# Seven block products in both ConvGLU layers, with sums of weight blocks formed by adding transfers

## The chip, the core and the metric

The kernel runs on one core of a Trainium2 chip. A core has five engines with a queue each: PE (TensorE, matrix products), DVE (VectorE), ACT (ScalarE), POOL (GpSimd) and SP (SyncE, which here only issues transfers). Each queue is worked off in order; engines wait for one another through semaphores. Operands lie in SBUF (128 partitions), products land in PSUM (eight banks of 128 x 512 float32). The metric is the device time of one execution in microseconds. Three runs of the kernel before gave 1870.25, 1871.61 and 1875.65, median 1871.61.

## What is computed

A two-layer diffusion backbone on 512 latent tokens and 256 context tokens of width 1024. Layer 0 mixes tokens with windowed attention, layer 1 with a bidirectional gated recurrence (HGRN2), and each layer ends in a ConvGLU, which is what the change touches:

```python
def conv_glu(h, w_up, conv_w, conv_b, w_down):
    gate, val = jnp.split(h @ w_up, 2, axis=-1)
    return (jax.nn.silu(dwconv3(gate, conv_w, conv_b)) * val) @ w_down
...
        hx2 = rms_norm(x, norm2_g[layer]) * (1.0 + sc2) + sh2
        x = x + g2 * conv_glu(hx2, ffn_w_up[layer], ffn_conv_w[layer], ffn_conv_b[layer], ffn_w_down[layer])
        if not last:
            ctx = ctx + cg1 * yc
...
            ctx = ctx + cg2 * conv_glu(hc2, ffn_w_up[layer], ffn_conv_w[layer], ffn_conv_b[layer], ffn_w_down[layer])
    return x
```

`w_up` is 1024 x 5632 (2816 gate columns and 2816 value columns), `w_down` 2816 x 1024. Layer 0 works on latent and context tokens, layer 1 on latent tokens only. All is float32.

## The kernel before

Features lie on partitions, tokens along the free dimension. To keep float32 accuracy with the faster float32r products, every operand is split into a high and a low part: ACT rounds a copy (`wh`, `hn[:, 0]`), DVE subtracts it from the source (`wl`, `hn[:, 1]`), and PE forms three products, high-high, high-low and low-high (`mm_steps`, L170; `product`, L188).

Weights come through `load_raw` (L90): SP transfers them into a tile `wr` of 2048 float32 a partition, of which there are two buffers, shared by all weight loads and by the 1 MB pieces of `ada_w` (`ada_steps`, L306). Split parts go to slots of `operand` (L84): 512 columns each, from a rotation of pools. In layer 0's ConvGLU these are `ws0` (4 slots) and `wsC` (2); in layer 1's `ws0` 4, `wsC` 2, `wsD` 2 and `wsE` 2.

The ConvGLU (`ffn`, L958) goes in rounds of hidden tiles of 128 (L31: six rounds in layer 0, three of 8, 7 and 7 in layer 1; 22 tiles in each layer). In a round, `up` (L973) makes each hidden tile's gate and value, multiplies, convolves and gates; one tile of the next round is made ahead; then the round's tiles go through `w_down` (L1006 to L1023). In layer 0 `up` also draws one step of the `ada_w` product for layer 1 (`side`).

Layer 0 uses a scheme of seven block products in place of eight (Winograd's form of Strassen's): `load_pair` (L125) treats the 1024 x 256 weight block of a hidden tile as 2 x 2 blocks: `a11`, `a12` (gate columns, inner features 0 to 511 and 512 to 1023), `a21`, `a22` (value columns, likewise). DVE forms four sums (`total`, L136): s1 = a21 + a22, s3 = a11 - a21, s2 = s1 - a11, s4 = a12 - s2, the last three in place in `wr`, s1 in the tile `s1` of pool `tmpA`, which has one buffer (two in layer 1's pool `tmpB`). Seven operands of 512 columns are split (L140, L141). The activations are split in two token halves of 386, and `halves` and `combos` (L365, L384) make seven operand sets `hs` from sums of their blocks, done when the residual stream is complete. `gate_pair` (L914) runs the seven products of 12 matmuls each (4 inner tiles, 3 part products), in the order 0, 1, 3, 6, 2, 5, 4 (0, 1, 3, 2, 4, 6, 5 for the first tile), into three PSUM banks Z, Y and V, copies intermediate sums out with ACT, adds with DVE (L925), and multiplies by the row factor `R` on DVE and, for the value half, on POOL (L926).

Layer 1 uses plain products (`gate_plain`, L898): for gate and value each eight inner tiles, three part products and two column ranges (256 and 258 tokens), 96 matmuls a hidden tile, with four split operands a tile from `load_w` (L99) and activations scaled and split once (`scaled`, L355, called from `hgrn_out`, L1274). Its multiplications by `R` are four DVE instructions that read PSUM (L912).

The order of the instructions on each engine comes from a planner, which simulates the program; `high_priority(offset=W_AHEAD)` lets the weight preparation run ahead of its place in the program.

Of the kernel before, what the change touches and what calls it, by code (L numbers as in the profile page):

```python
# [68 lines left out]
def f(t):  # L69
    return t.bitcast(F32)  # L70


class Kernel:
# [51 lines left out]
    def load_pair(self, parts, tmp):  # L125


        nc = self.nc
        raw, n = self.load_raw(parts)
        q = n // 4  # L130
        a11, a12, a21, a22 = (raw[:, i * q:(i + 1) * q] for i in range(4))
        s1 = tmp.tile([P, 512], F32, tag="s1", name="s1")[:, 0:q]
        ops = [tuple(t[:, 0:q] for t in self.operand()) for _ in range(7)]

        def total(o, x, y, op):
            nc.vector.tensor_tensor(o, x, y, op=op)  # L136
            return o

        def parts(i, src):
            nc.scalar.activation(ops[i][0], src, AF.Copy)  # L140
            nc.vector.tensor_tensor(ops[i][1], src, f(ops[i][0]), op=ALU.subtract)  # L141


        with self.tc.high_priority(offset=W_AHEAD):
            parts(0, a11)
            parts(1, a12)
            total(s1, a21, a22, ALU.add)
            s3 = total(a21, a11, a21, ALU.subtract)
            s2 = total(a11, s1, a11, ALU.subtract)
            parts(3, s2)  # L150
            parts(6, s3)
            parts(2, s1)
            parts(5, a22)
            s4 = total(a12, a12, s2, ALU.subtract)
            parts(4, s4)
        return ops
# [227 lines left out]
    def combos(self, ys, kk, hs, late=False):  # L384

        nc = self.nc
        (b11, b12), (b21, b22) = ys

        def put(i, src):
            nc.scalar.activation(hs[i][:, 0, kk], src, AF.Copy)  # L392
            nc.vector.tensor_tensor(hs[i][:, 1, kk], src, f(hs[i][:, 0, kk]), op=ALU.subtract)

        def diff(o, x, y, eng=nc.vector):
            eng.tensor_tensor(o, x, y, op=ALU.subtract)
            return o

        if late:
            t3 = diff(b22, b22, b12)  # L400
            t4 = diff(b21, b21, b11, nc.gpsimd)
            put(5, diff(b21, t4, t3))
# [114 lines left out]
    def row_factor(self, acc, lat_only, tmp, pp, tag, width, R, sh, dg):  # L517
# [18 lines left out]
        if R.shape[1] > TW:  # L536
            nc.vector.memset(R[:, TW:], sh)

# [358 lines left out]

    def gate_plain(self, ft, ops, hn, G, gg, R, rows, half, tmp, bank):  # L898


        nc = self.nc
        act = lambda k: (hn[:, 0, k], hn[:, 1, k])
        cols = ((0, 256), (256, C0))
        for j, dst in enumerate((G[:, 1:1 + C0], gg)):
            ps = [bank("pd")[:, 0:hi - lo] for lo, hi in cols]
            for _ in self.mm_steps(ops[j], range(KT), act, [(o, lo) for o, (lo, _) in zip(ps, cols)]):
                pass
            for _ in rows:
                pass

            for o, (lo, hi) in zip(ps, cols):
                nc.vector.tensor_tensor(dst[:, lo:hi], o, R[:, lo:hi], op=ALU.mult)  # L912

    def gate_pair(self, ft, ops, hs, G, gg, R, rows, half, tmp, bank):  # L914
# [10 lines left out]
        add = lambda o, x, y: nc.vector.tensor_tensor(o, x, y, op=ALU.add)  # L925
        times = lambda eng, o, x, y: eng.tensor_tensor(o, x, y, op=ALU.mult)  # L926
# [6 lines left out]
        nc.scalar.activation(g[2], Z, AF.Copy)  # L933
        next(rows, None)
        if ft == 0:
# [13 lines left out]
        add(g[3], g[3], t2)  # L949
        add(g[2], g[2], V)  # L950
# [7 lines left out]
    def ffn(self, l, hs, R, rows, lat_only, tmp, acp, bk, gp, done, side=None):  # L958
        nc, a = self.nc, self.a
        wup, wdn = a["ffn_w_up"][l], a["ffn_w_down"][l]  # L960
        half = C0 // 2 if lat_only else hs[0].shape[3]
# [11 lines left out]
        def up(ft):  # L973

            ws_ = [self.wcols(wup, ft * P, P), self.wcols(wup, DFF + ft * P, P)]
            ops = self.load_w(ws_) if lat_only else self.load_pair(ws_, tmp)
# [5 lines left out]
            (self.gate_plain if lat_only else self.gate_pair)(ft, ops, hs, G, gg, R, rows, half, tmp, bank)  # L982
# [291 lines left out]
    def hgrn_out(self, part, hn, acc, tmp, pj):  # L1274
        nc = self.nc
        self.shifts(1, 1, hn)
        wout = self.a["hgrn_w_out"][0]
        oh = part[0]
        act = lambda k: (oh[:, 0, k], oh[:, 1, k])
        for dp in range(KT // 2):  # L1280
# [6 lines left out]
            for j in range(2):  # L1287
# [14 lines left out]
    def run(self, stop=99):  # L1302
# [80 lines left out]
        self.hgrn_out(part, hn, acc, ot, pj)  # L1383
# [3 lines left out]
        R = Rp.tile([P, C0], F32, tag="R", name="R2")  # L1387
# [23 lines left out]
        self.ffn(1, hn, R, rows, True, tmp, acp, bk, gp, done1)  # L1411
# [41 lines left out]
```

## Time and profile before

| what | value |
|---|---|
| median of the three runs | 1871.61 us |
| the profiled execution, device time | 1872.88 us |
| its span in the profile | 1871.1 us |
| granted TensorE clock, mean | 0.988 |
| layer 0's ConvGLU | 425 to 970 us of the span |
| layer 1's ConvGLU | 1481 to 1871 us |

The span is what the profile's rows add up to; 1.8 us of the execution lie outside it. The rows used here are those of the page (busy time by engine, the chain of work that ended last, groups of instructions, transfers with the median time from issue to landing), the list of that chain in order of time, the timeline of single queues, and busy times of each engine in chosen stretches of the span. A row of a group has the line, engine, operation, output and inputs, shape and count, then busy time in us, mean ns of one, and the idle time before them with what ended it.

### The profile page before, as it was taken

Reading aid. Unit: us, or ns where it says so; the run is one execution under the profiler, and the core shown is the slowest. Engines: PE = TensorE matmul, PEld = TensorE weight load, DVE = VectorE, ACT = ScalarE, POOL = GpSimd, SP = SyncE. Lnnn points to the kernel's source line nnn. Section 1 sums busy time; section 2 is a strip of 40 time slices with the busy share of each in tenths; the row PEclk is TensorE's granted clock in tenths of the full one; section 3 lists DMA queues with packets and bytes.
Section 4 is the critical chain, followed back from the end, with each engine's and each line's share of the span. In section 5 each row is a group of like instructions: output and inputs, shape, how many; then the busy total and the mean of one; then the engine's idle time right before and its main releaser. Section 6 shows DMA issues by size and latency. Waiting matters only on the chain.

```text
span 1871.1 us, 32302 instructions
## 1 busy us (share of the span) xinstructions
PE 1801.3 (96%) x13326; PEld 1576.9 (84%) x13326; DVE 1214.1 (65%) x2243; ACT 754.7 (40%) x1478; POOL 247.4 (13%) x233
## 2 busy tenths in 40 slices
PE   6999999998999999999998999999998999999998
PEld 4976786787888888989887888988886799899997
DVE  5575667466867686766777676777676655455462
ACT  4354555465534252434354333333332443233332
POOL 1233333103201000101013101111110200000000
PEclk9999999998999999999998999999999999999999
DMA  9204104232333333233313212122220332333321
GB/s 309 66 23 158 47 24 169 68 102 68 124 113 102 113 124 113 91 113 124 113 61 90 58 35 58 35 57 58 57 69 24 90 91 91 90 96 96 92 82 65
DMA packets 204416, 166.44 MB, mean 89 GB/s; under 512 B 5149, under 2 KB 198254, under 8 KB 199150
## 3 DMA queue, kind: packets, MB, share of 16 engines
q1 hardware_dynamic: 196608, 160.47, 27.8%
q10 hardware_dynamic: 7662, 3.92, 0.7%
q8 instruction: 105, 1.72, 0.4%
q14 instruction: 41, 0.34, 0.1%
HBM read 162.27 MB, written 2.10 MB: 88 GB/s over the span
## 4 chain that ended last, share of the span: by engine, by line
PE 87%; DVE 5%; DMA 4%; issue 2%; ACT 1%; POOL 1%; SPq 0%; ACTq 0%; POOLq 0%; DVEq 0%
PE dn L170 15%; PE pd L170 13%; PE pZ L188 8%; PE pf L170 8%; PE pV L188 4%; PE pjq L598 4%; PE pv L170 4%; PE ao L170 4%; PE ho L170 3%; PE pq L170 3%; PE pv L824 2%; PE pt L816 2%; PE ada L309 2%; PE pY L188 2%; PE pgate L170 2%; PE kv L598 2%
## 5 line engine op out<-in xcount | busy, mean ns | idle before, releaser
L117 ACT ACTIVATE wh<-wr 128x512 fp32r<-128x512 f32 (+1 forms) x320 | 193.0, 618 | 452.3 <-DMA wr<-in_ffn_w_up 74.8
L118 DVE TENSOR_TENSOR wl<-wr,wh 128x512 fp32r<-128x512 f32 (+1 forms) x320 | 223.6, 705 | 140.3 <-ACT wh L117 138.3
L170 PE MATMUL dn<-g,wh 128*128 128x512 f32 (+1 forms) x1056 | 263.3, 357 | 2.2 <-ACT g L995 2.2
L170 PE MATMUL pd<-hn,wh 128*128 128x256 f32 (+1 forms) x1408 | 227.3, 284 | 0.9 <-issue 0.9
L170 PEld LDWEIGHTS dn<-g,wh 128*128 128x128 f32 x1056 | 175.4, 189 | 32.7 <-ACT g L995 2.8
L170 PEld LDWEIGHTS pd<-hn,wh 128*128 128x128 f32 x1408 | 194.2, 190 | 2.5 <-issue 2.3
L188 PE MATMUL pZ<-hs,wh 128*128 128x386 f32 x704 | 185.2, 345 | 3.0 <-ACT wh L140 1.5
L170 PE MATMUL dn<-g,wl 128*128 128x512 f32 (+1 forms) x528 | 159.4, 356 | 0.0
L140 ACT ACTIVATE wh<-wr 128x512 fp32r<-128x512 f32 x132 | 81.6, 628 | 167.9 <-DMA wr<-in_ffn_w_up 47.4
L170 PE MATMUL pd<-hn,wl 128*128 128x256 f32 x704 | 141.8, 283 | 0.0
L188 PEld LDWEIGHTS pZ<-hs,wh 128*128 128x128 f32 x704 | 128.0, 190 | 15.7 <-ACT wh L140 4.4
L141 DVE TENSOR_TENSOR wl<-wr,wh 128x512 fp32r<-128x512 f32 x132 | 94.0, 717 | 53.6 <-ACT wh L140 53.5
L170 PE MATMUL pf<-hn,wh 128*128 128x512 f32 (+1 forms) x512 | 119.3, 349 | 9.7 <-DVE xc L1023 8.8
L188 PE MATMUL pZ<-hs,wl 128*128 128x386 f32 x352 | 119.4, 343 | 2.2 <-DVE wl L141 2.2
L926 POOL TENSOR_TENSOR gg<-gg,R 128x772 f32<-128x772 f32 x22 | 53.9, 2449 | 458.3 <-DVE gg L925 446.6
L170 PEld LDWEIGHTS pd<-hn,wl 128*128 128x128 f32 x704 | 109.0, 190 | 0.0
L1023 DVE SCALAR_TENSOR_TENSOR xl<-dn,mod,xl 128x512 f32<-128x512 f32 x72 | 53.9, 748 | 73.7 <-PE dn L170 73.6
L170 PEld LDWEIGHTS dn<-g,wl 128*128 128x128 f32 x528 | 87.4, 188 | 14.8
L170 PEld LDWEIGHTS pf<-hn,wh 128*128 128x128 f32 x512 | 80.9, 192 | 22.5 <-ACT wh L117 9.1
L188 PE MATMUL pV<-hs,wh 128*128 128x386 f32 x352 | 92.2, 341 | 5.0 <-ACT hs L392 5.0
L598 PE MATMUL pjq<-wh,hn 128*128 128x256 f32 x384 | 77.8, 291 | 0.0
L188 PEld LDWEIGHTS pZ<-hs,wl 128*128 128x128 f32 x352 | 66.7, 190 | 6.6 <-DVE gg L925 3.4
(299 smaller groups left out, 3807.1 us busy)
## 6 DMA issues: line engine op xcount, KB each, us to landing
wr<-in_ffn_w_up SPq DMA_DIRECT2D x88, 512.0 KB, 5.1
wada<-in_ada_w SPq DMA_DIRECT2D x40, 1024.0 KB, 4.8
wr<-in_hgrn_w_in SPq DMA_DIRECT2D x40, 512.0 KB, 4.2
ar<-in_ada_w SPq DMA_DIRECT2D x32, 256.0 KB, 7.1
wr<-in_ffn_w_down SPq DMA_DIRECT2D x16, 512.0 KB, 4.1
wr<-in_ffn_w_down SPq DMA_DIRECT2D x8, 896.0 KB, 4.7
wr<-in_attn_w_in SPq DMA_DIRECT2D x6, 1024.0 KB, 8.1
wr<-in_attn_w_out SPq DMA_DIRECT2D x8, 512.0 KB, 4.9
```

The costliest lines, as they stand in the source:

```text
L117: nc.scalar.activation(wh, src, AF.Copy)
L118: nc.vector.tensor_tensor(wl, src, f(wh), op=ALU.subtract)
L140: nc.scalar.activation(ops[i][0], src, AF.Copy)
L141: nc.vector.tensor_tensor(ops[i][1], src, f(ops[i][0]), op=ALU.subtract)
L170: nc.tensor.matmul(o, lhsT=wt, rhs=at[:, t0:t0 + o.shape[1]], start=(first and n == 0 and i == 0), stop=(last and n == len(ks) - 1 and i = ...
L188: self.nc.tensor.matmul(ps, lhsT=wt, rhs=at, start=(first and k == 0 and i == 0), stop=(k == nk - 1 and i == 2), skip_group_check=not first)
L309: nc.tensor.matmul(ps[32 * j:32 * j + 32, 0:512], lhsT=self.cs[:, k, :], rhs=raw[:, j * 512:(j + 1) * 512], start=(k == 0), stop=(k == KT ...
L598: nc.tensor.matmul(out, lhsT=x, rhs=y[:, wk], start=(start and k == 0 and j == 0), stop=(stop and k == KT - 1 and j == 2))
L816: nc.tensor.transpose(pt[:, j * P:(j + 1) * P], pr[j][:, b * P:(b + 1) * P], self.ident)
L824: nc.tensor.matmul(pv[a * HD:(a + 1) * HD, 0:256], lhsT=V[:, tl, g, :], rhs=pT[:, a * 256:(a + 1) * 256], start=(b == 0), stop=(b == len(t ...
L926: times = lambda eng, o, x, y: eng.tensor_tensor(o, x, y, op=ALU.mult)
L1023: nc.vector.scalar_tensor_tensor(x[:, d], o, self.modc(l, v, 5, d), x[:, d], op0=ALU.mult, op1=ALU.add)
```

## The change

`load_pair` no longer uses DVE for the four sums. SP loads the block `a11` a second time, into the tile that was s1's and is now called `s3`, and POOL issues four transfers from SBUF to SBUF that add to their destination, each of 128 x 512 float32:

```diff
-        s1 = tmp.tile([P, 512], F32, tag="s1", name="s1")[:, 0:q]
+        s3 = tmp.tile([P, 512], F32, tag="s1", name="s3")[:, 0:q]
...
-        def total(o, x, y, op):
-            nc.vector.tensor_tensor(o, x, y, op=op)
+        def more(o, x):
+            nc.gpsimd.dma_start(out=o, in_=x, accum_op=ALU.add)
             return o
...
-            parts(0, a11)
-            parts(1, a12)
-            total(s1, a21, a22, ALU.add)
-            s3 = total(a21, a11, a21, ALU.subtract)
-            s2 = total(a11, s1, a11, ALU.subtract)
-            parts(3, s2)
-            parts(6, s3)
-            parts(2, s1)
-            parts(5, a22)
-            s4 = total(a12, a12, s2, ALU.subtract)
-            parts(4, s4)
+            nc.sync.dma_start(out=s3.rearrange("p (k m) -> p k m", m=P), in_=parts[0][:, 0:4])
+            parts_(0, a11)
+            parts_(1, a12)
+            more(s3, a21)
+            s1 = more(a21, a22)
+            s2 = more(a11, s1)
+            parts_(3, s2)
+            parts_(6, s3)
+            parts_(2, s1)
+            parts_(5, a22)
+            s4 = more(a12, s2)
+            parts_(4, s4)
```

Only sums are formed (s3 = a11 + a21, s1 = a21 + a22, s2 = a11 + s1, s4 = a12 + s2): the second row of blocks enters with its sign turned. The signs are put right on the side of the activations and of the results: `put` in `combos` takes a factor for operands 2 and 3 and two differences are turned round, and `gate_pair` copies two results with a factor of -1 and subtracts where it added:

```diff
-        put(2, t1)
+        put(2, t1, -1.0)
         t2 = diff(b22, b22, t1)
-        put(3, t2)
+        put(3, t2, -1.0)
         yield
-        put(5, diff(b21, b21, t2))
+        put(5, diff(b21, t2, b21))
...
-        nc.scalar.activation(g[2], Z, AF.Copy)
+        nc.scalar.activation(g[2], Z, AF.Copy, scale=-1.0)
...
-        add(g[3], g[3], t2)
-        add(g[2], g[2], V)
+        less(g[3], t2)
+        less(g[2], V)
```

Layer 1 takes the same scheme, with token halves of 258 (514 columns and two of padding). `gate_plain` goes; `hgrn_out` makes the seven operand sets instead of the one split of the activations:

```diff
-        half = C0 // 2 if lat_only else hs[0].shape[3]
+        half = hs[0].shape[3]
...
-            ws_ = [self.wcols(wup, ft * P, P), self.wcols(wup, DFF + ft * P, P)]
-            ops = self.load_w(ws_) if lat_only else self.load_pair(ws_, tmp)
+            ops = self.load_pair([self.wcols(wup, ft * P, P), self.wcols(wup, DFF + ft * P, P)], tmp)
...
-            (self.gate_plain if lat_only else self.gate_pair)(ft, ops, hs, G, gg, R, rows, half, tmp, bank)
+            self.gate_pair(ft, ops, hs, G, gg, R, rows, half, tmp, bank)
...
-        self.shifts(1, 1, hn)
...
+            some.append(self.combos(self.halves(1, 1, dp, 258, True, tmp, ("y0", "y1"), 4), dp, hs))
+            next(some[-1])
             for d in (dp, dp + 4):
-                self.scaled(1, 1, d, hn, True)
                 self.square_acc(d, acc, True, tmp, "sg", first=(d == 0), eng=nc.gpsimd)
+        for rest in some:
+            for _ in rest:
+                pass
...
-        hn = self.hn_tile(hc, "hn3", C0)
+        hs1 = hc.tile([P, 7, 2, 4, 258], F32R, tag="hs", name="hs3")
+        hs = [hs1[:, i] for i in range(7)]
...
-        R = Rp.tile([P, C0], F32, tag="R", name="R2")
+        R = Rp.tile([P, 516], F32, tag="R", name="R2")
```

The row factor's padding columns are filled in layer 1 too. Rounds, pools, the number of `wr` buffers and the priorities stay as they were.

More of the change, by code (lines that the diff above doesn't have):

```diff
@@ L131, in load_pair, with parts_ @@
         a11, a12, a21, a22 = (raw[:, i * q:(i + 1) * q] for i in range(4))
-        s1 = tmp.tile([P, 512], F32, tag="s1", name="s1")[:, 0:q]
+        s3 = tmp.tile([P, 512], F32, tag="s1", name="s3")[:, 0:q]
         ops = [tuple(t[:, 0:q] for t in self.operand()) for _ in range(7)]
-        def total(o, x, y, op):
-            nc.vector.tensor_tensor(o, x, y, op=op)
+        def more(o, x):
+            nc.gpsimd.dma_start(out=o, in_=x, accum_op=ALU.add)
             return o
-        def parts(i, src):
+        def parts_(i, src):
             nc.scalar.activation(ops[i][0], src, AF.Copy)
@@ L389, in combos, with put @@
         (b11, b12), (b21, b22) = ys
-        def put(i, src):
-            nc.scalar.activation(hs[i][:, 0, kk], src, AF.Copy)
-            nc.vector.tensor_tensor(hs[i][:, 1, kk], src, f(hs[i][:, 0, kk]), op=ALU.subtract)
+        def put(i, src, sign=1.0):
+            nc.scalar.activation(hs[i][:, 0, kk], src, AF.Copy, scale=sign)
+            if sign > 0:
+                nc.vector.tensor_tensor(hs[i][:, 1, kk], src, f(hs[i][:, 0, kk]), op=ALU.subtract)
+            else:
+                nc.vector.scalar_tensor_tensor(hs[i][:, 1, kk], src, sign, f(hs[i][:, 0, kk]), op0=ALU.mult, op1=ALU.subtract)
         def diff(o, x, y, eng=nc.vector):
@@ L401, in combos @@
             t4 = diff(b21, b21, b11, nc.gpsimd)
-            put(5, diff(b21, t4, t3))
+            put(5, diff(b21, t3, t4))
             put(6, t3)
@@ L535, in row_factor @@
         nc.vector.memset(R[:, SH:C0], sh)
-        if R.shape[1] > TW:
-            nc.vector.memset(R[:, TW:], sh)
+        if R.shape[1] > TW or lat_only:
+            nc.vector.memset(R[:, C0 if lat_only else TW:], sh)
     def spread(self, r, nt, out, tmp, tag="dg"):
@@ L895, in add_gated @@
             self.nc.vector.scalar_tensor_tensor(x[:, d], ps[:, lo:hi], self.modc(l, v, which, d), x[:, d], op0=ALU.mult, op1=ALU.add)
[L898 to L912, printed above, removed]
     def gate_pair(self, ft, ops, hs, G, gg, R, rows, half, tmp, bank):
@@ L925, in gate_pair @@
         add = lambda o, x, y: nc.vector.tensor_tensor(o, x, y, op=ALU.add)
+        less = lambda o, x: nc.vector.tensor_tensor(o, o, x, op=ALU.subtract)
         times = lambda eng, o, x, y: eng.tensor_tensor(o, x, y, op=ALU.mult)
@@ L939, in gate_pair @@
             prod(6, V, True)
-            nc.scalar.activation(g[3], V, AF.Copy)
+            nc.scalar.activation(g[3], V, AF.Copy, scale=-1.0)
             prod(5, V)
@@ L943, in gate_pair @@
             prod(6, V, True)
-            nc.scalar.activation(g[3], V, AF.Copy)
+            nc.scalar.activation(g[3], V, AF.Copy, scale=-1.0)
             prod(2, Z)
@@ L1272, in hgrn, with hgrn_out @@
         return part
-    def hgrn_out(self, part, hn, acc, tmp, pj):
+    def hgrn_out(self, part, hs, acc, tmp, pj):
         nc = self.nc
-        self.shifts(1, 1, hn)
         wout = self.a["hgrn_w_out"][0]
@@ L1279, in hgrn_out @@
         act = lambda k: (oh[:, 0, k], oh[:, 1, k])
+        some = []
         for dp in range(KT // 2):
@@ L1379, in run @@
         hc = self.pool(rs, "hC", 1, right=True)
-        hn = self.hn_tile(hc, "hn3", C0)
+        hs1 = hc.tile([P, 7, 2, 4, 258], F32R, tag="hs", name="hs3")
+        hs = [hs1[:, i] for i in range(7)]
         ot = self.pool(es, "ot", 1)
         acc = Rp.tile([P, LAT], F32, tag="acc", name="acc2")
-        self.hgrn_out(part, hn, acc, ot, pj)
+        self.hgrn_out(part, hs, acc, ot, pj)
         if stop == 4:
@@ L1409, in done1 @@
                 nc.sync.dma_start(out=a["out"][0, :, (d - 1) * P:(d + 1) * P].rearrange("(t p) c -> p t c", p=P), in_=ost[0])
-        self.ffn(1, hn, R, rows, True, tmp, acp, bk, gp, done1)
+        self.ffn(1, hs, R, rows, True, tmp, acp, bk, gp, done1)
         es.close()
```

## The prediction, made before the changed kernel was run

> **What bounds the kernel now.** The page first: busy times by engine and the chain that ended last.
>
> ```profile
> span 1871.1 us, 32302 instructions
> PE 1801.3 (96%) x13326; PEld 1576.9 (84%) x13326; DVE 1214.1 (65%) x2243; ACT 754.7 (40%) x1478; POOL 247.4 (13%) x233
> ...
> PE 87%; DVE 5%; DMA 4%; issue 2%; ACT 1%; POOL 1%; SPq 0%; ACTq 0%; POOLq 0%; DVEq 0%
> ```
>
> PE is on 87% of the chain. What the change can gain is therefore PE work, and it takes some only in layer 1. The chain in order of time shows that layer (start, us, what):
>
> ```profile
> 1492.16 98.39 PE pd L170 x816
> 1590.55 44.23 PE dn L170 x192
> 1634.78 80.50 PE pd L170 x672
> 1715.28 38.60 PE dn L170 x168
> 1753.88 69.00 PE pd L170 x576
> ```
>
> No wait stands between these pieces: layer 1's gate and value products (`pd`) run at PE's pace, 80.50 / 672 = 0.120 us a matmul, 11.5 us for a tile's 96. Busy times by stage agree (stage, PE, PEld, DVE, ACT, POOL, clock, DMA share, GB/s):
>
> ```profile
> 425.00:970.00 545.00, 531.93 (x3003) 477.71 (x3002) 391.52 (x660) 224.43 (x403) 69.65 (x42) 0.99 0.34 107
> 1410.00:1480.00 70.00, 61.13 (x370) 46.34 (x369) 45.87 (x72) 24.49 (x47) 10.10 (x7) 0.93 0.22 61
> 1480.00:1492.00 12.00, 8.70 (x60) 7.57 (x60) 4.44 (x9) 3.01 (x5) 2.30 (x2) 0.92 0.31 89
> 1634.00:1715.00 81.00, 81.00 (x676) 80.88 (x675) 47.32 (x95) 30.24 (x48) 0.00 (x0) 1.00 0.29 87
> ```
>
> In the fourth stage PE never stops; weights come early enough. SP's waits in layer 1 (waited for: us, times, longest) say what paces the loads:
>
> ```profile
> SPq L95 <- DVE wl L118: 314.8, 30, 16.4
> ```
>
> A load waits for the last split of the tile whose `wr` buffer it takes. The two buffers are the resource on which this change leans. In layer 0 (first row of the stages) PE idles only 545 - 531.9 = 13.1 us. SP's timeline there:
>
> ```profile
> 533.85 0.99 SPq L95 DMA_DIRECT2D wr<-in_ffn_w_up  x2
> 540.90 0.34 SPq L307 DMA_DIRECT2D wada<-in_ada_w  x1
> 550.87 0.99 SPq L95 DMA_DIRECT2D wr<-in_ffn_w_up  x2
> 560.70 0.34 SPq L307 DMA_DIRECT2D wada<-in_ada_w  x1
> 566.66 0.99 SPq L95 DMA_DIRECT2D wr<-in_ffn_w_up  x2
> ```
>
> Up loads follow one another after 17.0 and 15.8 us, mean 16.4.
>
> **The change, part by part.**
>
> *Products of layer 1.* 84 matmuls a tile in place of 96, the shape hardly changed (258 columns for 256 and 258). 12 x 22 x 0.120 = **-31.6 us**, if the operands are there every 84 x 0.120 = 10.1 us.
>
> *DVE in layer 1*, from the groups of the stage 1634 to 1715:
>
> ```profile
> L118 DVE TENSOR_TENSOR wl<-wr,wh 128x512 fp32r<-128x512 f32 x25 | 17.2, 686 | 13.1 <-ACT wh L117 13.1
> L989 DVE SCALAR_TENSOR_TENSOR u<-G,par,u 128x512 f32<-128x512 f32 x7 | 5.3, 752 | 0.2
> L992 DVE SCALAR_TENSOR_TENSOR gg<-gg,u 128x512 f32<-128x512 f32 x6 | 4.5, 747 | 0.0
> L996 DVE TENSOR_TENSOR g<-gg,g 128x512 fp32r<-128x512 f32 x6 | 4.2, 693 | 4.2 <-ACT g L995 4.2
> L912 DVE TENSOR_TENSOR G<-pd,R 128x258 f32<-128x258 f32 x7 | 2.9, 418 | 0.0
> L985 DVE TENSOR_SCALAR cb<-G,wsum,par 128x1 f32<-128x1 f32 x7 | 1.9, 267 | 0.0
> L983 DVE COPY G<-G 128x1 f32<-128x1 f32 x7 | 1.0, 149 | 0.0
> ```
>
> A new tile needs seven splits (4.80), five half-width additions or multiplications (2.09), two `u` steps (1.50), 0.75, 0.69 and 0.42: 10.3 us, just above PE's 10.1. So DVE becomes the next bound at 10.3. ACT: four more copies, three more splits; far from full at 30.24 of 81.
>
> *The adding transfers.* No transfer of this trace is issued by POOL or adds. Its price X, from POOL's issue until the next may go, decides everything. Nearest rows (KB each, us from issue to landing):
>
> ```profile
> wr<-in_ffn_w_up SPq DMA_DIRECT2D x88, 512.0 KB, 5.1
> ...
> ar<-in_ada_w SPq DMA_DIRECT2D x32, 256.0 KB, 7.1
> wr<-in_ffn_w_down SPq DMA_DIRECT2D x16, 512.0 KB, 4.1
> ...
> wr<-in_ffn_w_down SPq DMA_DIRECT2D x8, 384.0 KB, 2.9
> ...
> xs<-in_x ACTq DMA_DIRECT2D x8, 256.0 KB, 2.7
> ```
>
> One adds 256 KB, which means reading 512 KB and writing 256. Below it stands 2.7 (a plain 256 KB), beside it 4.1 (512 KB both ways), above it 7.1 (256 KB in the crowd of the start). I take the middle of 2.7 and 4.1, 3.4, and 0.2 for the wait between two: **X = 3.6 us**, an estimate.
>
> The Trainium skill (DMA: Bandwidth & Descriptors, section "Anatomy of one DMA — SWDGE (gpsimd) path") fits a POOL-issued transfer by 2.0 us plus bytes over 436 KB per us: about 2.6 us here, an estimate from that page, for a copy; no run here shows it yet. By it the time would be that of the first rival below.
>
> The four depend on one another: s3 reads a21 before s1 overwrites it, s2 reads s1, s4 reads s2. A `wr` buffer is therefore held for 5.1 (loads) + 1.0 (the second copy of a11 behind them; 384 to 512 KB is 1.2 apart) + 4X + 1.3 (last split, 0.63 on ACT, 0.69 on DVE) + 1.0 (waits in ACT's, DVE's and SP's queues, my estimate) = 8.4 + 4X = 22.8 us. Two buffers: one tile every **11.4 us**, against PE's 10.1 and 11.5 before. That gives back 1.34 us for each of 19 tiles (22 less one a round, prepared under the `dn` pieces): **+25.5 us**.
>
> *Layer 0.* DVE loses its four sums:
>
> ```profile
> L136 DVE TENSOR_TENSOR wr<-wr 128x512 f32<-128x512 f32 x44 | 32.7, 746 | 0.4
> L136 DVE TENSOR_TENSOR wr<-s,wr 128x512 f32<-128x512 f32 x22 | 15.3, 696 | 0.2
> L136 DVE TENSOR_TENSOR s<-wr 128x512 f32<-128x512 f32 x22 | 15.2, 689 | 2.4 <-DMA wr<-in_ffn_w_up 2.3
> ```
>
> 63.2 us of an engine that is 72% busy there and ends little of PE's 13.1 us of idling: **-2**. Against that, `tmpA` has one buffer for s3: the next tile's extra load waits on SP for `parts_(6, s3)`, and the `ada_w` pieces wait behind it. The ring is 0.5 (issue) + 2.7 (256 KB) + 3X + 2.6 (splits 3 and 6) = 16.6 us at X = 3.6, against the 16.4 at which up loads follow now: 0.2 x 16 tiles (22 less one a round) = **+3**. Signs cost nothing: a factor in an ACT copy, a subtraction for an addition.
>
> *Start of layer 1.* SP's first up load and PE's first product:
>
> ```profile
> 1474.71 72.11 SPq L95 DMA_DIRECT2D wr<-in_ffn_w_up  x14
> ...
> 1480.96 0.72 PE L170 MATMUL pd<-hn,wh 128*128 128x256 f32 x4 [0.89 <-issue]
> ```
>
> Operand 3 needs s2: 1474.7 + 6.1 + 3X + 1.3 = 1492.9. PE has two products (24 x 0.120) until 1483.8 and then waits 9.1 us; today's 3.3 us of idling before the row factor (1480 to 1492) lie inside that: **+6**. The seven activation sets need 11 half-width DVE steps in each of four groups, 18.4 us, for 16 instructions as this one:
>
> ```profile
> L363 DVE SCALAR_TENSOR_TENSOR hn<-xl,gs,hn 128x512 fp32r<-128x512 f32 x16 | 19.9, 1245 | 0.2 <-ACT hn L362 0.2
> ```
>
> Half of that row lies in `hgrn_out`, 10 us. The other 8 lie under DVE's idle 24 us (45.87 of 70, above); only the last group shows: **+2**.
>
> *POOL's order.* The value multiplication comes to POOL in layer 1:
>
> ```profile
> L926 POOL TENSOR_TENSOR gg<-gg,R 128x772 f32<-128x772 f32 x22 | 53.9, 2449 | 458.3 <-DVE gg L925 446.6 <-DVE hn L423 11.7
> ```
>
> At 516 columns 1.64 us. It waits for a tile's last product, and an adding transfer queued behind it waits too; its other neighbour, the previous transfer, does the same to it, which delays only `w_down`. I let one chain in two lose 1.64 us, halved by the two buffers: 0.41 x 19 = **+8**.
>
> **Sum**: -31.6 + 25.5 - 2 + 3 + 6 + 2 + 8 = +10.9 on the profiled execution's 1872.9 (span 1871.1 and 1.8 outside; 1.3 above the median of the runs): **1884 us**. Around it, each microsecond of X counts 2 x 19 + 3 x 16 + 3 = 89 us. No change lies at X = 3.48.
>
> **Rivals.** (1) *Short transfers: faster.* At X = 2.7 the hold is 19.2 us, 9.6 a tile, and DVE's 10.3 sets the pace: +0.2 x 19 = 4; layer 0's ring 13.9 is under its 16.4; start +3.3, activations +2, DVE -2: -24.3, 1849 us. It needs X below 3.4. For it: 2.7 and 2.9 are in the trace, and the sources lie in SBUF. Against: twice the reads, and a load in flight 29% of the time. The skill's 2.6 us would end here too, since DVE binds. (2) *Long transfers.* At X = 4.75: 1872.9 + 10.9 + 1.15 x 89 = 1986; at 5.1, the row of up loads, 2017. For it: loads of 256 KB took 7.1 in a crowd. (3) *POOL serves one chain at a time*: if the planner queues a tile's four transfers together, each waiting for the one before, a tile takes 4X + 1.64 = 16.0 us. In layer 1 that is 5.9 x 19 = 112 in place of 25.5 + 8: 1963 us. Layer 0's 16.4 hardly notices. Two buffers half a hold apart speak for mixing, the queue in order against it.
>
> **Chances.** Forecast (X 3.4 to 4.2, chains mixed) 0.36, of which 0.03 ends faster and 0.11 within 0.3% (5.6 us, about what a measurement of this kernel can tell from no change); (1) 0.34; (2) 0.20; (3) 0.10. Faster 0.37, same 0.11, slower 0.52. The range runs from X = 2.7 and a little less, 1845, to X = 4.75, 1985; it covers (3) and leaves out the longer half of (2).
>
> **What would show it.** Right: `pZ`, `pY`, `pV` in layer 1 at 0.120 us a matmul; PE idle there, ended by ACT splits that wait for POOL's transfers; SP's up loads some 11.4 us apart. For (1): PE without gaps, DVE near full. For (3): POOL's transfers in fours, never two chains in flight. Wrong altogether: PE gaps in layer 1 that end in `gg` or `hs`, or a slower layer 0 whose up loads still follow after 16.4 us.

## The result, and the profile after

The changed kernel took 1998.7 us (median of 4 runs, 1987.2 to 2003.9), the kernel before 1871.4 in runs beside it (1870.3 to 1875.7). The ratio is 1.067, interval 1.062 to 1.072: slower by about 127 us, and above the forecast's range.

The page of the kernel after (span, busy time by engine):

```profile
span 1995.0 us, 32786 instructions
...
PE 1823.5 (91%) x13062; PEld 1581.9 (79%) x13062; DVE 1248.2 (63%) x2278; ACT 816.9 (41%) x1666; POOL 418.3 (21%) x439
```

PE runs 264 matmuls less than before and is busy 22 us longer. The idle time of PE grew from 1871.1 - 1801.3 = 69.8 us to 171.5. Where this happened, the first product of `ho` (the mixing of layer 1, between the two ConvGLUs) tells. The matmuls of that tile in both kernels (duration in ns, then first and last start):

```profile
L170 PE MATMUL ho<-oh,wh x128: 388/396/794, 1412.5 to 1479.4; 128*128 128x512 f32 x128
```

```profile
L172 PE MATMUL ho<-oh,wh x128: 390/396/796, 1479.2 to 1546.0; 128*128 128x512 f32 x128
```

So 66.7 us are lost ahead of it, in layer 0, and 123.9 - 66.7 = 57.2 behind it, in layer 1. Below, "layer 0" is the start of the first `ho` matmul (1412.5 before), and "rest" is the span less that (458.6 before, 515.8 after). Busy times of the two stages, before and then after (stage, length, PE, PEld, DVE, ACT, POOL, clock, DMA share, GB/s); the stages start and end at the same work:

```profile
396.00:1003.80 607.80, 584.17 (x3305) 523.33 (x3303) 441.30 (x733) 261.68 (x482) 81.60 (x53) 0.99 0.33 103
1479.40:1871.10 391.70, 382.94 (x2685) 357.98 (x2683) 198.92 (x379) 129.35 (x206) 2.30 (x2) 0.99 0.29 87
```

```profile
396.00:1070.00 674.00, 607.62 (x3307) 538.80 (x3306) 395.52 (x645) 259.46 (x482) 147.51 (x141) 0.95 0.54 135
1546.00:1995.00 449.00, 381.05 (x2421) 348.10 (x2419) 278.60 (x486) 190.43 (x373) 109.70 (x113) 0.92 0.61 142
```

In layer 0 PE idles 66.4 us in place of 23.6 (+42.8), and the same number of matmuls keeps it busy 23.5 us longer, at a clock of 0.95. In layer 1 it idles 68.0 in place of 8.8 (+59.2); the 264 matmuls that went should have taken 31.6 us off 382.94, which makes 351.3, but 381.05 are there (+29.7), at a clock of 0.92. The balance is 42.8 + 23.5 + 59.2 + 29.7 - 31.6 = 123.6 us: with the 102 us of new gaps come 53 us of slower matmuls. The mean clocks of the two profiles, 0.988 and 0.962, say the same: 1995.0 x 0.038 - 1871.1 x 0.012 = 53 us of full clock lost.

What PE waits for in layer 0 (waited for: us in all, times, longest) and the groups of the page that stand around it:

```profile
PE pV L190 <- ACT wh L141: 18.5, 6, 5.0
PE pZ L190 <- ACT gg L923: 11.9, 5, 4.8
PE pZ L190 <- ACT t L919: 5.7, 1, 5.7
```

```profile
L141 ACT ACTIVATE wh<-wr 128x512 fp32r<-128x512 f32 x264 | 157.4, 624 | 316.2 <-DMA wr<-wr 231.1
...
L137 POOL DMA_DIRECT2D wr<-wr x132 | 115.6, 876 | 410.3 <-issue 95.4
...
wr<-wr POOLq DMA_DIRECT2D x132, 256.0 KB, 3.7
...
s<-wr POOLq DMA_DIRECT2D x44, 256.0 KB, 3.8
```

PE waits for splits, and ACT's splits sat idle 231 us for the adding transfers. The copies `gg` and `t` out of PSUM are short (under 0.5 us), but they stand behind such splits in ACT's queue, so PE waits for them too. A transfer lands 3.7 us after its issue, nearly the 3.6 us that the prediction took.

### The profile page after: what moved, and what is told of

It is laid out like the page before. It is cut to its first block, busy times and chain, and to the rows that moved or that the text cites. A ratio compares the mean times of both kernels' runs of the same rounds, so it can differ in the third digit from the quotient of the medians.

```text
span 1995.0 us, 32786 instructions
## 1 busy us (share of the span) xinstructions
PE 1823.5 (91%) x13062; PEld 1581.9 (79%) x13062; DVE 1248.2 (63%) x2278; ACT 816.9 (41%) x1666; POOL 418.3 (21%) x439
## 5 line engine op out<-in xcount | busy, mean ns | idle before, releaser
L190 PE MATMUL pZ<-hs,wh 128*128 128x386 f32 (+1 forms) x1408 | 335.4, 329 | 76.5 <-ACT wh L141 35.6
L142 DVE TENSOR_TENSOR wl<-wr,wh 128x512 fp32r<-128x512 f32 x264 | 205.7, 795 | 221.1 <-ACT wh L141 220.3
L190 PEld LDWEIGHTS pZ<-hs,wh 128*128 128x128 f32 x1408 | 250.8, 202 | 97.6 <-ACT wh L141 41.0
L190 PE MATMUL pZ<-hs,wl 128*128 128x386 f32 (+1 forms) x704 | 225.6, 325 | 2.4 <-DVE wl L142 2.3
L137 POOL DMA_DIRECT2D wr<-wr x132 | 115.6, 876 | 410.3 <-issue 95.4
L190 PE MATMUL pV<-hs,wh 128*128 128x386 f32 (+1 forms) x704 | 166.9, 326 | 27.6 <-ACT wh L141 19.4
L190 PEld LDWEIGHTS pV<-hs,wh 128*128 128x128 f32 x704 | 125.6, 200 | 33.1 <-ACT wh L141 21.5
L190 PE MATMUL pV<-hs,wl 128*128 128x386 f32 (+1 forms) x352 | 114.5, 325 | 2.2 <-DVE wl L142 2.2
L916 POOL TENSOR_TENSOR gg<-gg,R 128x772 f32<-128x772 f32 (+1 forms) x44 | 81.7, 1856 | 149.0 <-DVE gg L915 149.0
L172 PEld LDWEIGHTS pf<-hn,wh 128*128 128x128 f32 x512 | 80.3, 191 | 22.5 <-ACT wh L117 9.1
L190 PE MATMUL pY<-hs,wh 128*128 128x386 f32 (+1 forms) x352 | 85.3, 329 | 2.5 <-ACT wh L141 2.4
L1012 DVE SCALAR_TENSOR_TENSOR xl<-dn,mod,xl 128x512 f32<-128x512 f32 x72 | 53.7, 746 | 40.1 <-PE dn L172 40.0
```

Of the source, the lines that this page charges most:

```text
L137: nc.gpsimd.dma_start(out=o, in_=x, accum_op=ALU.add)
L172: nc.tensor.matmul(o, lhsT=wt, rhs=at[:, t0:t0 + o.shape[1]], start=(first and n == 0 and i == 0), stop=(last and n == len(ks) - 1 and i = ...
L190: self.nc.tensor.matmul(ps, lhsT=wt, rhs=at, start=(first and k == 0 and i == 0), stop=(k == nk - 1 and i == 2), skip_group_check=not first)
L1012: nc.vector.scalar_tensor_tensor(x[:, d], o, self.modc(l, v, 5, d), x[:, d], op0=ALU.mult, op1=ALU.add)
```

## Experiments

All times are medians of at least four runs beside runs of the kernel before; ratios are to those runs. They are told in groups that answer one question; here they are together:

| kernel | us | ratio (95%) | layer 0 | rest |
|---|---|---|---|---|
| before | 1871.4 to 1878.6 | 1 | 1412.5 | 458.6 |
| after | 1998.7 | 1.067 (1.062 to 1.072) | 1479.2 | 515.8 |
| change in layer 0 alone | 1941.2 | 1.035 (1.032 to 1.037) | 1475.2 | 459.9 |
| transfers in layer 1 alone | 1927.2 | 1.028 (1.025 to 1.032) | 1417.7 | 502.4 |
| all sums on DVE | 1892.8 | 1.009 (1.007 to 1.012) | 1418.0 | 475.7 |
| no adding transfers | 1864.5 | 0.996 (0.993 to 0.998) | 1408.4 | 452.5 |
| last transfer only | 1873.5 | 0.999 (0.998 to 1.000) | 1414.2 | 455.0 |
| first transfer only | 1891.1 | 1.009 (1.007 to 1.010) | 1432.0 | 461.9 |
| s3 on DVE, three transfers | 1931.3 | 1.029 (1.027 to 1.032) | 1440.6 | 493.3 |
| transfers of half width | 1939.7 | 1.034 (1.031 to 1.036) | 1452.4 | 489.5 |
| gg on DVE | 1993.5 | 1.063 (1.061 to 1.066) | 1470.6 | 516.6 |
| chain of three | 1991.6 | 1.061 (1.058 to 1.064) | 1482.6 | 512.8 |
| third `wr` buffer in layer 1 | 2003.7 | 1.067 (1.065 to 1.070) | 1479.7 | 524.4 |
| operand slots in another rotation | 2005.2 | 1.067 (1.065 to 1.070) | 1498.9 | 507.8 |
| filler matmuls | 2052.5 | 1.094 (1.092 to 1.096) | 1511.3 | 537.5 |
| sums that nobody reads | 2016.7 | 1.073 (1.070 to 1.076) | 1493.5 | 525.1 |
| the same, two chains of half width | 1909.4 | 1.018 (1.015 to 1.021) | 1434.6 | 472.9 |
| before, other rotation of slots | 1865.0 | 0.993 (0.992 to 0.995) | 1401.0 | 462.6 |
| layer 1 in seven products, DVE sums | 1893.9 | 1.008 (1.007 to 1.010) | 1413.6 | 477.3 |
| the same, other rotation of slots | 1874.1 | 0.998 (0.997 to 0.999) | 1401.3 | 471.7 |

### Which part costs: the two layers, and the transfers

The first is the kernel before with `load_pair`, `combos` and `gate_pair` of after (layer 1 stays in plain products).

> Layer 0 with adding transfers, layer 1 as before. By the traces layer 0 alone lost 66 us (the first ho matmul moved from 1412.5 to 1479.2 us). Theory A, each layer loses by itself because its own weight chain is late: 1871 + 66 = 1937 us, up loads in layer 0 some 20 us apart. Rival, the loss in layer 0 is made by what layer 1 needs (other pools, an order planned for the whole program): under 1900 us.

The second is the kernel after with layer 0's sums on DVE and without the second load there (one part of the edit):

```diff
+            if self.on_dve:
+                nc.vector.tensor_tensor(o, o, x, op=ALU.add)
+            else:
+                nc.gpsimd.dma_start(out=o, in_=x, accum_op=ALU.add)
```

> Layer 0 with its four sums on DVE, layer 1 seven products with adding transfers. Theory A: layer 0 back to 1412 us at the first ho matmul, layer 1 keeps its loss of 57 us: 1871 + 57 = 1928 us. Rival, layer 1's loss comes from what layer 0 leaves behind: under 1895 us.

They cost 66 and 52 us, 119 of the 127 together: the layers lose independently of each other. The same switch set for both layers takes all sums back to DVE and leaves the second load out:

> Seven products in both layers, all sums on DVE, no second load of a11. Theory A: nothing is lost in layer 0; in layer 1 DVE needs 10.3 + 4 x 0.72 = 13.2 us a tile against PE's 10.1, so it sets the pace: 1871 + (13.2 - 11.5) x 19 + 8 = 1911 us. Rival, DVE's queue runs ahead under the dn pieces and the seven products show: 1845 us.

1892.8 lies between: with DVE's sums the seven products lose too, most of it in layer 1 (rest 475.7 for 458.6). And with the transfers left out:

```diff
-            nc.gpsimd.dma_start(out=o, in_=x, accum_op=ALU.add)
             return o
```

> The changed kernel with the four adding transfers left out (the sums are not formed), the second load of a11 kept. Theory A, the wait for the chain of adding transfers is the whole loss: layer 1 at DVE's 10.3 us a tile, layer 0 as before: about 1850 us. Rival, the seven-product scheme in layer 1 or the single buffer of s3 with its extra load costs by itself: above 1880 us.

1864.5, between the two expectations: the adding transfers cost 134 us. Without any price for the sums (the second load is still made) the seven products bring only 6.1 us from the first `ho` matmul on, 4.1 of them in the ConvGLU. That stage without the adds:

```profile
1473.40:1861.00 387.60, 361.05 (x2421) 331.71 (x2419) 273.27 (x484) 193.81 (x376) 34.04 (x26) 0.98 0.36 105
```

PE's busy time falls by 382.94 - 361.05 = 21.9 us in place of 31.6, and its idle time grows from 8.8 to 26.6. Even free sums would not have brought the forecast's gain.

### What in the transfers costs: four candidates

First, POOL's own work in front of them:

```diff
-        times(nc.gpsimd, gg, gg, R)
+        times(nc.vector, gg, gg, R)
```

> The kernel after, with the multiplication gg by R moved from POOL to DVE in both layers (44 instructions of 2.2 or 1.6 us taken out of POOL's queue, about 1 us each put on DVE). Theory O (order: the four transfers of a tile stand one behind the other in POOL's queue and gg, which waits 149 us in all for DVE, stands between them): the transfers no longer wait behind gg, and the time falls by 40 us or more, to 1960 or less. Rival R (the chain of four dependent transfers is long by itself, whatever else is in the queue): 1990 to 2010, within 15 us of the kernel after.

Measured 1993.5, ratio 1.063 for 1.067: about 6 us, but the two intervals overlap, and DVE has the multiplications instead. `gg` is not the cause.

Second, the small tile's ring, by taking s3 back to DVE (its load goes too):

```diff
-            nc.sync.dma_start(out=s3.rearrange("p (k m) -> p k m", m=P), in_=parts[0][:, 0:4])
...
-            more(s3, a21)
+            nc.vector.tensor_tensor(s3, a11, a21, op=ALU.add)
```

> The kernel after, with the second load of a11 and the transfer of s3 left out and s3 = a11 + a21 formed by DVE in the same small tile (one DVE sum more per tile, about 0.7 us; three adding transfers left). Theory B (the one buffer of s3, whose load waits for the split of the tile before, closes the ring that sets the pace): most of the loss goes, to 1900 to 1920. Theory R (the length of the chain: four steps become three, a quarter of the 134 us that the adds cost): about 1965. If neither ring nor length matters, only what is in flight of the last steps: 1990 or more.

1931.3, half of the loss gone, 38.6 us of it in layer 0 (one small buffer) and 22.5 in layer 1 (two): more than a quarter, less than all. Third, the length of one transfer:

```diff
-            nc.gpsimd.dma_start(out=o, in_=x, accum_op=ALU.add)
+            nc.gpsimd.dma_start(out=o[:, 0:256], in_=x[:, 0:256], accum_op=ALU.add)
```

> The kernel after with the four adding transfers of half the columns (256 of 512; the other half of each sum is left out). If the step is mostly its fixed part (about 2.9 of 3.7 us stay): the time falls by a fifth of 134 us, to about 1970. If it goes by bytes: by half, to about 1930. The order of POOL's queue and all waits stay as they are.

1939.7, and the price of a transfer in the kernel after and in this one (least, median, most):

```profile
DMA to landing us min/median/max: 3.2/3.7/8.1
```

```profile
DMA to landing us min/median/max: 2.6/2.9/7.3
```

0.8 us less a transfer takes away 59 us, 26.8 and 26.3 of the profiled span in the two layers: 66 us for each microsecond of X (53.1 / 0.8; the prediction had 89). The expectation's two cases part here: a transfer lost little more than a fifth of its time, as in the first, but the kernel 59 of 134 us, as in the second. So the loss is not in proportion to a transfer's time, and this run, which halves the bytes too, does not say why. Fourth, the number of dependent steps: the second load takes a21, so that two sums don't wait for each other.

```diff
-            more(s3, a21)
-            s1 = more(a21, a22)
+            s3 = more(a21, a11)
+            more(s1, a22)
             s2 = more(a11, s1)
```

> The kernel after with the second load taken of a21 instead of a11, so that s3 = a21 + a11 is added in place and s1 = copy + a22 beside it: the same four transfers and the same sums, but a chain of three dependent steps in place of four. Theory R (length of the dependent chain): a quarter of 134 us less, about 1965. Theory B (the ring through the one small buffer): the small tile is now held until s2's transfer has read it, so 1995 or more. Theory O (POOL's queue in order, each transfer behind the one before): the second of the pair starts without a wait, a little less, 1970 to 1985.

1991.6, within the noise of the kernel after (their intervals overlap). The small tile is held longer here, until s2's transfer has read it, so this run alone does not clear the length of the chain. And a second transfer in flight is slower; the copy's transfer, second of the pair, in the issues of this kernel:

```profile
s<-wr POOLq DMA_DIRECT2D x44, 256.0 KB, 5.3
```

One of the four transfers alone, first the one through the small tile, then the last:

```diff
-            more(s3, a21)
+            more(s3, a21, True)
```

```diff
-            s4 = more(a12, s2)
+            s4 = more(a12, s2, True)
```

(in both, `more` issues only where told `True`)

> The kernel after with only the first of a tile's four adding transfers (s3 = copy of a11 + a21) and its second load; the sums s1, s2 and s4 are left out. Without any adds it took 1864.5, with all four 1998.7. Theory B (the ring of the one small buffer in layer 0: load, transfer, split, next load): most of its cost stands in layer 0, the first ho matmul at 1425 or later (1408.4 without adds, 1479.2 with all), and under 5 us in layer 1, where there are two such buffers: 1880 to 1895. Theory L (every transfer costs a quarter): 1898, half of it in each layer. Theory K (only the chain, one transfer behind the other, costs): 1865 to 1872.

> The kernel after with only the last of the four adding transfers (a12 + a11 in place of s4); the sums s3, s1 and s2 are left out, the second load stays. One transfer a tile that waits for no other transfer, 88 us of transfer time less than a chain of four in each layer. Theory K (only the chain costs, since one transfer fits into the time by which a tile runs ahead): 1865 to 1875. Theory L (every transfer costs a quarter of 134 us): 1898.

The first costs 27 us, 23.6 of the span in layer 0, as theory B has it (and 9.4 in layer 1, more than the 5 that it allowed); the last 9, 5.8 of it in layer 0. If the parts add up, the single small buffer is thus worth some 18 us of layer 0's 66, an estimate. The chain of four costs 134 us, more than four times the dearer of the two.

### Is it the wr buffers, the slots, or gaps that feed on themselves?

A third buffer, in layer 1 (not shown: rounds of 7, 7 and 8 tiles, and one buffer less in the pool `gpB`, which make the room):

```diff
-        raw = self.wp.tile([P, 2048], F32, tag="wr", name="wr")
+        wp = self.wps[0]
+        self.wps = self.wps[1:] + self.wps[:1]
+        raw = wp.tile([P, 2048], F32, tag="wr", name="wr")
...
+        self.wps = [self.wp, self.wp, self.pool(es, "wpE", 1)]
```

> The kernel after with a third wr buffer in layer 1 (rounds of 7, 7, 8 tiles in place of 8, 7, 7, which frees the room for it); layer 0 as it is. Theory H (in layer 1 the hold of a wr buffer, 27.7 us for two tiles' worth, sets the pace: a third buffer makes it 9.2 us a tile, under PE's 10.1): the time from the first ho matmul to the end falls from 515.8 to 475 or less, the kernel to 1960 or less. Theory Q (the queues' order: splits on ACT that wait for a transfer stand ahead of copies out of PSUM for which PE waits, and POOL's transfers stand behind those of the other tile): 500 or more, the kernel 1985 or more.

No gain: rest 524.4 for 515.8. What POOL's transfers waited for in layer 1, after and with the third buffer (us, times):

```profile
  DMA wr<-in_ffn_w_up: 53.9, 12
  DVE wl L142: 47.0, 15
...
  DMA wr<-wr: 32.0, 15
```

```profile
  DVE wl L144: 73.3, 20
  DMA wr<-wr: 55.7, 16
  DMA wr<-in_ffn_w_up: 49.1, 8
```

The load is hardly less waited for, and the wait for the transfer ahead and for splits grew instead. The hold of a `wr` buffer, the prediction's bound, is not what binds by itself. More operand slots, by drawing twice a turn on the pool of four:

```diff
         self.wsp.append(self.pool(top, "wsC", 2))
+        self.wsp.append(self.ws0)
```

> The kernel after with the operand slots taken in another rotation: the pool of four slots is drawn on twice a turn, the pools of two once, so that a slot comes round after 6 operands in place of 4 in layer 0 and after 10 in place of 8 in layer 1; no memory is added. Theory S (a tile's s2 waits for the split of a11, which waits for a slot that PE still reads, so the number of slots fixes how early the chain of transfers starts): 30 us or more faster, 1965 or less, with gains in both layers. Theory Q (the queue of POOL and the length of the chain, whatever the slots): 1985 or more. The small buffer's ring in layer 0 stays in both.

2005.2: neither. And filler matmuls in front of the product that waits for s2:

```diff
+        self.product(V, ops[0], lambda k: (hs[0][:, 0, k], hs[0][:, 1, k]), 4, True)
         prod(3, Z)
```

> The kernel after with twelve more matmuls a tile, whose sum is overwritten (a second product of operand 0 into the bank that product 6 starts anew), put ahead of product 3, which waits for s2: 22 x 12 x 0.18 = 48 us of PE work in layer 0 and 22 x 12 x 0.12 = 32 us in layer 1. Theory G (each gap of PE costs twice, since the granted clock is low for some us behind it: the gap itself and slow matmuls after it): the fillers lie in gaps and keep the clock up, so the granted clock rises from 0.962 to 0.975 or more, and the time stays at 1990 to 2010 for 80 us more work. Rival (the clock has another cause): the clock stays at 0.96, and the time rises by a third of the work or more, to 2025 and above.

Measured 2052.5, in the rival's range, at clocks of 0.964 to 0.970, between the two (0.957 to 0.964 after): 54 of about 80 us of added work show. PE's idle time fell only from 171.5 to 2048.8 - 1888.9 = 159.9 us (span less PE's busy time), so the fillers hardly went into the gaps, and the run does not say what filled gaps would do to the clock.

### Reading the sums, or making them?

In the next run the second load and the number of transfers stay, but no split reads a sum; all four transfers go into the small tile:

```diff
-            more(s3, a21)
-            s1 = more(a21, a22)
-            s2 = more(a11, s1)
-            parts_(3, s2)
...
-            s4 = more(a12, s2)
-            parts_(4, s4)
+            for x in (a21, a22, a11, a12):
+                more(s3, x)
+            parts_(3, a11)
...
+            parts_(4, a12)
```

> The kernel after with the same second load and the same number of adding transfers, one behind the other (copy += a21, += a22, += a11, += a12, all into the small tile), but no split reads a sum: the operands of s2, s3, s1 and s4 are split from a11, a21, a21 and a12, so the sums are left out. The transfers still hold the wr buffers and POOL's queue, and the small buffer still closes its ring. Theory D (what costs is that splits wait for the end of a chain, and behind them on ACT and DVE the rest of the tile): the time falls to 1885 or less. Theory T (throughput: four transfers in series, 14 to 16 us a tile, hold POOL and the wr buffers longer than PE's 10.1 in layer 1 and near its 15.6 in layer 0, whoever reads the sums): 1950 or more, with up loads of layer 1 still some 14 us apart.

2016.7, as slow as the kernel after though no operand waits for a sum, with four up loads of layer 1 in 1657.57 - 1603.95 = 53.6 us (SP's timeline), 13.4 a tile. So transfers made one behind the other are enough for the whole loss, as theory T has it. That waiting for sums costs nothing in the kernel after does not follow, since this kernel waits elsewhere. Its small tile is held by all four transfers, and SP's second load in layer 1 waits for that (waited for: us, times, longest), after and here:

```profile
SPq L146 <- DMA s<-wr: 44.2, 8, 8.4
```

```profile
SPq L146 <- DMA s<-wr: 236.3, 19, 19.4
```

POOL's queue in layer 0 of this kernel, and SP's (start us, us, what):

```profile
598.42 0.88 POOL L137 DMA_DIRECT2D s<-wr  x1 [4.14 <-DMA s<-in_ffn_w_up]
602.29 0.86 POOL L137 DMA_DIRECT2D s<-wr  x1 [3.00 <-DMA s<-wr]
605.86 0.85 POOL L137 DMA_DIRECT2D s<-wr  x1 [2.71 <-DMA s<-wr]
609.38 0.85 POOL L137 DMA_DIRECT2D s<-wr  x1 [2.67 <-DMA s<-wr]
```

```profile
594.83 0.37 SPq L146 DMA_DIRECT2D s<-in_ffn_w_up  x1
595.42 0.34 SPq L307 DMA_DIRECT2D wada<-in_ada_w  x1
612.63 0.37 SPq L146 DMA_DIRECT2D s<-in_ffn_w_up  x1
613.22 18.38 SPq L95 DMA_DIRECT2D wr<-in_ffn_w_down  x4
```

Load, four transfers of 3.5 to 3.9 us, next load: 612.63 - 594.83 = 17.8 us a tile, with what SP has behind it (`w_down` here) waiting too. Before, up loads followed after 16.4. With one small tile in layer 0, this is that tile's ring, closed by four transfers. Then the same with two chains of half width:

```diff
-            for x in (a21, a22, a11, a12):
-                more(s3, x)
+            for i, x in enumerate((a21, a22, a11, a12)):
+                more(s3[:, i % 2 * 256:i % 2 * 256 + 256], x[:, 0:256])
```

> As the run before this one (no split reads a sum, the sums are left out), with transfers of half the columns that go by turns into the left and the right half of the small tile: the bytes of the half-width run (1939.7), but two chains of two in place of one chain of four, so that POOL may have two in flight. Theory P (POOL's queue, which waits for each landing before it issues the next, is what is full): about 2 x 3.9 = 7.8 us of POOL's queue a tile in place of 4 x 2.9 = 11.6, under PE's 10.1, so 1875 to 1905. Theory D (the bytes on the DMA engines): as the half-width run, 1930 to 1955.

1909.4, between the two and nearer theory P. POOL's wait for the transfer ahead in layer 1, with one chain of four and with two chains of two (after, it was 25.4 + 32.0 = 57.4):

```profile
  DMA s<-wr: 165.0, 59
```

```profile
  DMA s<-wr: 37.3, 26
```

With two chains and half the bytes most of this wait is gone, and the kernel is 107 us faster than the one before it here. Against the half-width run, with as many bytes, it is 30 us faster, but not by this wait. There POOL's transfers waited in layer 1 for:

```profile
  DVE wl L142: 63.6, 18
  DMA wr<-wr: 23.5, 12
  DMA s<-wr: 16.6, 10
```

23.5 + 16.6 = 40.1 us for a transfer ahead, nearly the 37.3 here, but 63.6 for splits, which must have read a block before a transfer adds to it in place; here no transfer waits for a split. So the 30 us speak for a price of the sums in place as well: transfers that wait for splits, splits that wait for sums, or both. No run parts these. A half-width transfer lands after 3.2 us here (median), where one at a time took 2.9.

### A version that beats both

Two questions were left: do slots bind the kernel before, and do layer 1's seven products pay with DVE's sums? The first has the rotation edit above, nothing else:

> The kernel before with the same other rotation of the operand slots, nothing else. Its PE idles 13 us in layer 0 and hardly in layer 1, so by theory S there is little to gain: 1864 to 1876. By theory Q the same. A gain of over 6 us would say that slots bind before, too.

1865.0, 0.7% or 13.5 us faster than the kernel before beside it (1878.6): the forecast of little to gain was wrong. The first `pf` matmul, the end of layer 0's ConvGLU, before and with the rotation:

```profile
L170 PE MATMUL pf<-hn,wh x512: 276/389/763, 1003.8 to 1376.7; 128*128 128x512 f32 x86, 128*128 128x258 f32 x85
```

```profile
L170 PE MATMUL pf<-hn,wh x512: 276/388/767, 993.3 to 1365.6; 128*128 128x512 f32 x86, 128*128 128x258 f32 x85
```

10.5 us up to there, in layer 0, where a slot now comes round after six operands in place of four; from the first `ho` matmul on, this profile is 4.0 us longer. The second takes after's layer 1 with the `load_pair`, `combos` and `gate_pair` of before; then the rotation is added to it.

> Layer 0 as in the kernel before; layer 1 with the seven products, its sums by DVE and the signs of before; no adding transfer, no second load. With the signs of after in both layers this took 1892.8, 5.5 of it more in layer 0 than before. If those 5.5 us come from the signs and the order of the sums: 1884 to 1890. If they come from what is shared: 1890 or more.

> The kernel of the run before this one with the other rotation of operand slots as well. DVE has four sums a tile more in layer 1 (about 2.8 us on 10.3), over PE's 10.1, so DVE sets the pace there, and slots help little: 1880 to 1890 by theory Q. By theory S, the waits of PE for late splits go: 1865 to 1875, near or below the kernel before.

1893.9, by its median as slow as with the signs of after (its layer 0 is back at 1413.6, its rest no better), and with the rotation 1874.1: by slots, not by seven products, that kernel comes near the one before. Of the kernels that compute everything, the kernel before with the rotation is the fastest.

## Why the prediction was wrong, step by step

*The price of a transfer was right:* X = 3.6 forecast, 3.7 measured. It was the middle of two rows of plain transfers, so that it came out this near is partly luck. The runs show 3.7 us for 256 KB and 2.9 for 128. By the difference, 0.8 us for 128 KB, an adding transfer moves its bytes at about 160 KB per us and has 2.1 us that are fixed, an estimate from these two medians. The Trainium skill's fit (DMA: Bandwidth & Descriptors, section "Anatomy of one DMA — SWDGE (gpsimd) path") has 2.0 us and 436 KB per us, which makes about 2.6 and 2.3 us, estimates from that page: the fixed part agrees, the rate does not.

*The step that failed is "Two buffers: one tile every 11.4 us".* It let the chains of two tiles run side by side, each in its own `wr` buffer, held for 22.8 us. In the kernel after, SP's up loads of layer 1 (start, time over which the group of loads goes out):

```profile
1597.20 10.93 SPq L95 DMA_DIRECT2D wr<-in_ffn_w_up  x4
...
1624.92 11.31 SPq L95 DMA_DIRECT2D wr<-in_ffn_w_up  x4
...
1653.87 0.99 SPq L95 DMA_DIRECT2D wr<-in_ffn_w_up  x2
```

1653.87 - 1597.20 = 56.7 us for four tiles: 14.2 us a tile, against PE's 10.1. In the prediction's own sum the difference is 19 x (14.2 - 11.4) = 53 us, about the 47 by which layer 1 missed (57.2 for its -31.6 + 25.5 + 6 + 2 + 8 = 9.9). POOL's queue in that time:

```profile
1604.63 0.86 POOL L137 DMA_DIRECT2D s<-wr  x1
1608.16 0.85 POOL L137 DMA_DIRECT2D wr<-wr  x1 [2.68 <-DMA s<-wr]
1613.54 0.85 POOL L137 DMA_DIRECT2D s<-wr  x1 [4.52 <-DMA wr<-in_ffn_w_up]
1614.10 1.59 POOL L916 TENSOR_TENSOR gg<-gg,R 128x516 f32<-128x516 f32 x1
1615.33 1.20 POOL L137 DMA_DIRECT2D wr<-wr  x1
1617.64 0.85 POOL L137 DMA_DIRECT2D wr<-wr  x1 [1.11 <-issue]
1619.50 0.85 POOL L137 DMA_DIRECT2D wr<-wr  x1 [1.01 <-DMA wr<-wr]
```

By their order, the first two are s3 and s1 of one tile; its s2 goes at 1615.33, 7.2 us after s1, because s3 of the next tile stands ahead of it and waits 4.5 us for its own load; its s4 goes at 1619.50. The first tile's buffer is loaded anew after 1624.92 - 1597.20 = 27.7 us: 7.4 to the issue of s3, 18.6 from there to the landing of s4 (14.9 and 3.7), 1.7 to the next load, where the prediction had 6.1, 4X = 14.4 and 2.3. What was mis-sized is the chain in the middle. The chains mix in part, and still each waits for the other in the one queue. That is half of rival (3), priced at 16.0 us a tile and 1963 us and given a chance of 0.10: the queue in order costs, but (3)'s own sign, transfers in fours and never two chains in flight, is not in the trace. Where the prediction asked what binds once two buffers hold two chains, it named the buffers; a third one changed nothing, and transfers whose sums nobody reads cost as much.

*Layer 0 (-2 + 3) was the larger miss:* +66.7. "Layer 0's 16.4 hardly notices", said under rival (3), and the forecast with it took four transfers as shorter than a tile, but the queue also stands for the tile's load (93.7 us of POOL's idle time ahead of transfers in that stage), for splits of a tile's blocks (35.8) and for `gg`, beside 119.8 for the transfer ahead. 66.2 / 22 gives 3.0 us more a tile. The forecast's own ring of the small buffer, 0.2 us over 16.4, had no room in it for the split's wait; with one transfer alone it already showed (27 us against 9 for the transfer outside the ring).

*The gain of -31.6* came to 6.1 with free sums, because PE idles 17.8 us more there, and busy time falls by 21.9.

*Not in the sum at all:* the slower matmuls behind gaps, 23.5 + 29.7 = 53 us of the 124. *Start of layer 1 (+6), activations (+2)* were not measured apart. *POOL's order for gg (+8)* is not confirmed: some 6 us went with it, within the noise. That signs cost nothing holds in the medians: with DVE's sums 1892.8 with the signs of after, 1893.9 with those of before.

*Slope and constant.* The prediction's 89 us for each us of X stands against 66 measured; what was wrong is where the line crosses zero, forecast at X = 3.48. From 127 us at X = 3.7 and 66 us per us it would cross near 3.7 - 127 / 66 = 1.8 us, an estimate, below any transfer seen. Of the conditions for "right", PE idles, and splits that wait for transfers end it; but loads came after 14.2 in place of 11.4 us, and matmuls held 0.120 us only at full clock. Without the 14.2 the conditions could not tell the forecast from what happened.

*Open.* POOL's transfers fill 88 x 3.7 = 326 us of layer 1's 449, so the queue is not full all the time, and fillers on PE cost two thirds of their work. Which link closes the loop with the transfers (SP's order with the second load in it, the splits that wait for slots) was tried one link at a time, not two together; a second small tile in layer 0 was not tried. So that the adding transfers cost the 134 us is shown, and that they do so as a chain; how this splits between POOL's order, the small tile's ring and the waits between splits and sums in place is argued from the traces.

## What to carry to other kernels

A chain of transfers issued by one queue is a resource with a pace of its own: number times landing time, plus what the queue stands still for, against the pace of PE in each stage; here a third buffer behind the queue did not raise it. To tell waiting for a result from the cost of making it, keep the work and let nobody read it, and then look whether the rest still waits for the same things. And price gaps on PE above their length: in this kernel 53 us of slower matmuls came with 102 us of gaps.

## What was not expected of the hardware

The granted clock falls behind gaps, on one core, and recovers in microseconds. PE in layer 1 of the kernel after (start us, us, what, count; in brackets the idle time before):

```profile
1616.86 0.41 PE L190 MATMUL pV<-hs,wh 128*128 128x258 f32 x2
...
1619.67 1.32 PE L190 MATMUL pZ<-hs,wh 128*128 128x258 f32 x4 [2.29 <-ACT wh L141]
...
1622.49 0.63 PE L190 MATMUL pZ<-hs,wh 128*128 128x258 f32 x2
...
1623.20 0.40 PE L190 MATMUL pZ<-hs,wh 128*128 128x258 f32 x2
```

A pair takes 0.41 us before the gap, 0.63 after it, and 0.40 again from 1623.2 on, 3.5 us after PE started anew. In this trace the clock is either full or half, in stretches of 3.41 us. Three neighbouring ones (stretch, length, busy times of PE, PEld, DVE, ACT and POOL, clock, DMA share, GB/s):

```profile
1616.17:1619.59 3.42, 1.22 (x11) 1.01 (x9) 2.29 (x7) 1.84 (x4) 1.30 (x3) 1.00 0.67 112
1619.59:1623.00 3.41, 3.33 (x14) 3.18 (x15) 2.48 (x5) 1.80 (x4) 1.62 (x2) 0.50 1.10 201
1623.00:1626.41 3.41, 3.11 (x26) 2.91 (x26) 2.95 (x6) 2.87 (x6) 0.20 (x1) 1.00 0.53 98
```

PE is busy for 1.22 us of the first, 36%, and the second has half clock, though PE is busy for nearly all of it; then the clock is full again. In the whole trace of the kernel after, the clock falls from full to half 27 times, always behind a stretch with PE busy 56% or less. Of the 504 stretches behind which it stays full, none has PE busy under 50%. So in this trace a stretch of which PE uses about half or less lowers the clock of the next, and no single gap need be long. The Trainium skill (TensorE: Matmul & The Clock Gate, section "Part 1: The HAM clock gate (the "warmup" mystery)") tells of half clock after an idle window of about 3.4 us, and full clock after as long a busy one. The recovery agrees; for the fall the trace decides otherwise, since the gap here was 2.29 us, with one of 1.10 less than 2 us before it.

Of two adding transfers in flight the second is slower: 5.3 us (median) in place of 3.8.
